# Putting the Fourier stages and W_fourier between the head pairs of attention

## The chip, the cores and the metric

The kernel runs on one NeuronCore of one Trainium2 chip. The metric is the device time of one launch in microseconds; the median of three runs before the change is 1103.17 us (1102.57 to 1104.6).

## What is computed

The reference is a trunk of two layers. Each layer normalizes x (512 positions, 1024 channels), projects it once, and sends the result through two groups side by side: a Fourier group on 512 channels and windowed attention with 8 heads of 64 on 2 key heads. Their outputs are normalized, joined and projected with w_o; a feed-forward network with a short convolution follows. Everything is fp32.

```python
def fourier_mix(u, w_f, b_f):
    f = jnp.fft.fft2(u.astype(jnp.float32), axes=(1, 2), norm="ortho").real.astype(u.dtype)
    return f @ w_f + b_f

for l in range(DEPTH):
    h = rmsnorm(x, norm1[l])
    p = h @ w_in[l]                       # fourier 512 | q 8x64 | k 2x64 | v 2x64
    y_f = fourier_mix(u, w_fourier[l], b_fourier[l])
    q = rope(rmsnorm(q, q_norm[l]))
    k = rope(rmsnorm(k, k_norm[l]))
    y_a = windowed_gqa(q, k, v, sink[l])  # |i-j| <= 128, a sink logit per head
    mix = jnp.concatenate([rmsnorm(y_f, g_fourier_out[l]), rmsnorm(y_a, g_attn_out[l])], axis=-1)
    x = x + mix @ w_o[l]
    h = rmsnorm(x, norm2[l])
    up = dwconv_centred(h @ w_up[l], conv_w[l], conv_b[l])
    gate, val = up[..., :D_FF], up[..., D_FF:]
    x = x + (jax.nn.silu(gate) * val) @ w_down[l]
```

## The kernel before

x lies in SBUF with channels on the partitions, as eight tiles of 128 x 512. TensorE works on fp32r, so every operand is split into a high part (ScalarE, L86) and a low part (VectorE, L89 or L92), and `mm3` (L103 to L108) issues three matmuls for each product: high by high (L106), low by high (L107), high by low (L108). Weights of layer 0 are loaded raw (`wraw`, three buffers) and split on the way (`whi`, `wlo`, five buffers each). Those of layer 1 are split while layer 0 still runs (`presplit`, L135), through `m` and `tA` buffers, stored to DRAM as `kept`, and fetched ready split.

A layer's mixer has these steps, in the order of the program before:

- the projection to q, k, v; then `prep` and `turn_k`, `turn_q` for the keys and the fourth pair of heads (norm, RoPE, and transposes on PE, L423 and L434);
- the projection to the Fourier channels with `W_u` into four PSUM banks `pee` and `poo` (L495 to L511). The input is folded by the symmetry of the transform, so that cosine and sine parts have half the length;
- `prep` and `turn_q` for the other pairs, then `attention` for pairs 3, 0, 1, 2 (L513 to L517), a pair being heads 2p and 2p + 1;
- two Fourier stages (L534 to L566) as matmuls with the tables `th`, `tl` and the alternating row `altr` (L549, L551), each written out to `slab` tiles and a one-row `tail`;
- `W_fourier` (L568 to L597) in four column tiles: in layer 0 a load, a fold on DVE (`tA`), a split, 15 matmuls into `pu` and `pv`, bias on ACT (`tF`), unfolding on DVE, and squares summed in `accF`;
- the norm: `col_rstd` sums over the partitions on PE (L209) and takes the root with 12 small DVE ops (`nv`, `ni`, `nr`, `nq`); `row_rstd` spreads it over the partitions on PE (L216) and copies it to `rb`; then four scalings and four splits to `slab` (`ys`, L599 to L604);
- `w_o` on the Fourier half (96 matmuls, L624 to L627), the norm of the attention half, `w_o` on the attention half.

In `attention`, each head has four blocks of 128 queries. A block takes scores on PE (L459), mask and maximum on DVE (L463), the exponential on ACT, the reciprocal on DVE (L467), the scaling on POOL (L468), transposes on PE (L471) and a split to `pT`; a head ends with 12 matmuls by the values (`vz`). PSUM has eight banks: three `mm`, two `sc` (scores), two `tp` (transposes), one `av` (output). The `tA` ring has six buffers, shared by attention, the folds and `presplit`.

The framework fixes the order on each engine when the program is built: it takes instructions by their place in the program, but lets a later one pass where an earlier one still lacks operands or a buffer in its estimate. Each engine then runs its list strictly in order. Beside this, the matmuls of the Fourier half of `w_o` are tied to attention: the n-th product may not stand ahead of the (12 + n)-th block's transpose:

```python
after = steps[min(STEP0 + nfill[0] // RATE, 31)]
```

Of the kernel before, what the change touches and what calls it, by code (L numbers as in the profile page):

```python
# [37 lines left out]
def encoder_kernel(tc, t):  # L38
# [24 lines left out]
    def nm(s):  # L63
        uid[0] += 1
        return f"{s}_{uid[0]}"

    def f(x):
        return x.bitcast(F32)
# [6 lines left out]
    def psum(tag="mm"):  # L75
        return ps.tile([P, 512], F32, tag=tag, name=nm("ps"), bufs=BANKS[tag])
# [5 lines left out]
    def pair(tag, n=512):  # L82
        return temp(2 * n, tag, F32R).rearrange("p (s q) -> p s q", s=2)

    def act(out, in_, func=AF.Copy, **kw):
        return nc.scalar.activation(out, in_, func, **kw)  # L86
# [7 lines left out]
    def split(hi, lo, src, scale=None, eng=None):  # L94

        if scale is None:
            act(hi, src)
            tt(lo, src, f(hi), ALU.subtract, eng)
        else:
            act(hi, src, scale=scale)  # L100
            stt(lo, src, scale, f(hi), ALU.mult, ALU.subtract)
# [197 lines left out]
    def accum(tag="acc"):  # L299
        return cp.tile([P, 512], F32, tag=tag, name=nm(tag), bufs=1)  # L300
# [28 lines left out]
    for l in range(L):  # L329
# [87 lines left out]
        def turn_q(qs, tag):  # L417

            o = pair(tag)
            for h in range(2):  # L420
                pt = psum("tp")
                for b in range(NB):
                    nc.tensor.transpose(pt[:, b * P:(b + 1) * P], f(qs[:, b, h].rearrange("p s d -> p (s d)")), ident)  # L423
                act(o[:, h, :], pt)
            return o
# [67 lines left out]
        qT = {3: turn_q(qs3, "m4")}  # L493
# [16 lines left out]
                mm3(poo[:, 0:256], [h[:, s, 257:385] for s in range(2)], wo, st, sp_, skip_group_check=True)  # L510
                mm3(poo[:127, 256:512], [h[:, s, 385:512] for s in range(2)], wo, False, sp_, skip_group_check=True)  # L511

        for p, qs in enumerate(prep((0, 1, 2))):  # L513
            qT[p] = turn_q(qs, "act")
        attention(3, True)
        for p in range(3):
            attention(p, False)  # L517

        def tail_out(pe, scale):
            b = tp.tile([1, 2, 258], F32R, tag="tail", name=nm("tail"), bufs=2)  # L520
            split(b[:, 0, :], b[:, 1, :], pe[2][:1, :258], scale=scale)
            return b

        def stage_out(pe, po, scale):
            tiles = []
            for m in range(2):
                a = pair("slab", 514)
                n = P - m
                split(a[:, 0, :258], a[:, 1, :258], pe[m][:, :258], scale=scale)
                split(a[:n, 0, 258:514], a[:n, 1, 258:514], po[:n, m * 256:(m + 1) * 256], scale=scale)  # L530
                tiles.append(a)
            return tiles, tail_out(pe, scale)

        ue, ut = stage_out(pee, poo, 1.0)  # L534
        for stage in range(2):
            pe = [psum() for _ in range(2)]
            po = psum()
            pe.append(psum())
            for m, (c0, c1) in enumerate(((0, 128), (128, 256), (256, 257))):
                o = pe[m][:c1 - c0, :258]  # L540
                for i in range(2):
                    u2 = [ue[i][:, s, :] for s in range(2)]
                    if stage == 0:
                        mm3(o, [z[:, c0:c1] for z in u2], [z[:, 0:258] for z in tab[i]], i == 0, False)
                    else:
                        mm3(o, [z[:, c0:c1] for z in tab[i]], [z[:, 0:258] for z in u2], i == 0, False)
                for s in range(2):
                    if stage == 0:
                        nc.tensor.matmul(o, ut[:, s, c0:c1], altr, start=False, stop=s == 1)  # L549
                    else:  # L550
                        nc.tensor.matmul(o, altr[:, c0:c1], ut[:, s, :], start=False, stop=s == 1)  # L551
            for m in range(2):
                n = P - m
                o = po[:n, m * 256:(m + 1) * 256]
                for i in range(2):
                    kn = P - i
                    u2 = [ue[i][:kn, s, 258:514] for s in range(2)]
                    t2_ = [z[:kn] for z in tab[i]]
                    st = m == 0 and i == 0
                    if stage == 0:  # L560
                        mm3(o, [z[:, 1 + m * P:1 + m * P + n] for z in u2], [z[:, 256:512] for z in t2_],
                            st, i == 1, skip_group_check=True)
                    else:
                        mm3(o, [z[:, 257 + m * P:257 + m * P + n] for z in t2_], u2,
                            st, i == 1, skip_group_check=True)
            ue, ut = stage_out(pe, po, 1.0 if stage == 0 else 1.0 / 512.0)  # L566

        accF = accum("accF")  # L568
        yf = []
# [30 lines left out]
        for j in range(NF):  # L600
            stt(yf[j], yf[j], gF[:, l, j:j + 1], rbF, ALU.mult, ALU.mult)
            a = pair("slab")
            split(a[:, 0, :], a[:, 1, :], yf[j])
            ys.append(a)  # L604


        nfill = [0]
# [181 lines left out]
```

## Time and profile before

| | |
|---|---|
| median of three runs | 1103.17 us |
| profiled execution | 1104.05 us |
| its span, first to last instruction | 1102.2 us |
| mean granted clock of TensorE | 0.989 |
| PE busy | 1064.3 us, 97% |
| DVE busy | 786.7 us, 71% |
| ACT busy | 523.0 us, 47% |
| POOL busy | 87.9 us, 8% |
| DMA | 141.64 MB, 129 GB/s |

Times are microseconds from the start of the span. PE is TensorE's matmul, PEld its weight loads, DVE VectorE, ACT ScalarE, POOL GpSimd, SP the engine that issues the DMAs. A row of the timeline has start, duration, engine, line, operation, output and inputs, the count, and in brackets the idle time ahead of it with what ended it. A row of windows has, for a stretch, each engine's busy time with its count of instructions, then the granted clock, the share of the DMA engines and GB/s. Lines are those of the kernel before.

### The profile page before, as it was taken

The numbers are of one execution on the slowest core, as the hardware profiler recorded it, in microseconds if no ns is written. First come the engines' busy times: TensorE is split into PE (matmuls) and PEld (weight loads), VectorE is DVE, ScalarE is ACT, GpSimd is POOL, SyncE is SP. The second block draws the span as 40 slices with busy tenths as digits, with TensorE's granted clock in tenths as the row PEclk, the third lists the DMA queues.
The fourth block names the chain that finished last, engine by engine and source line by source line (L and its number), as shares of the span: only waits on it lengthen the run. The fifth ranks groups of instructions, "written<-read, shape, count | busy, mean of one in ns | idle before, by whom it ended". The sixth has DMA issues, their size and how long they took to land.

```text
span 1102.2 us, 14846 instructions
## 1 busy us (share of the span) xinstructions
PE 1064.3 (97%) x5187; PEld 891.9 (81%) x5187; DVE 786.7 (71%) x1574; ACT 523.0 (47%) x964; POOL 87.9 (8%) x158
## 2 busy tenths in 40 slices
PE   7988869999999999999999999999999999999998
PEld 7866757888888888888889888888888888888887
DVE  7898965878775867777736979476978435787732
ACT  5638842555454444555622677244554323455421
POOL 1014400000000000000000034000211000010100
PEclk9999969999999999999999999999999999999999
DMA  6312242233337973335955621323232332333241
GB/s 244 109 36 63 70 175 79 94 96 96 96 91 257 386 260 96 98 100 184 372 163 167 234 77 40 124 87 99 93 115 72 98 113 97 99 96 96 79 133 56
DMA packets 58573, 141.64 MB, mean 129 GB/s; under 512 B 6521, under 2 KB 19074, under 8 KB 58498
## 3 DMA queue, kind: packets, MB, share of 16 engines
q1 hardware_dynamic: 58498, 140.69, 39.4%
q8 instruction: 41, 0.67, 0.3%
q14 instruction: 34, 0.28, 0.1%
HBM read 117.60 MB, written 23.07 MB: 128 GB/s over the span
## 4 chain that ended last, share of the span: by engine, by line
PE 86%; DVE 8%; DMA 2%; ACT 2%; issue 1%; POOL 0%; SPq 0%; DVEq 0%; ACTq 0%
PE ps L106 28%; PE ps L108 27%; PE ps L107 27%; DVE tA L463 1%; DMA whi<-kept 1%; PE ps L459 1%; PE ps L471 1%; DVE wlo L89 1%; PE ps L216 1%; DVE pT L89 1%; DVE tF L92 1%; DVE act L89 1%; DMA wraw<-in_w_o_dram 1%; PE ps L209 1%; DVE tA L89 0%
## 5 line engine op out<-in xcount | busy, mean ns | idle before, releaser
L86 ACT ACTIVATE whi<-wraw 128x512 fp32r<-128x512 f32 (+1 forms) x296 | 181.6, 615 | 296.7 <-PE ps L108 283.2
L106 PE MATMUL ps<-act,whi 128*128 128x512 f32 x768 | 298.6, 389 | 0.0
L107 PE MATMUL ps<-act,wlo 128*128 128x512 f32 x768 | 298.6, 390 | 0.0
L108 PE MATMUL ps<-act,whi 128*128 128x512 f32 x768 | 298.0, 389 | 0.0
L89 DVE TENSOR_TENSOR wlo<-wraw,whi 128x512 fp32r<-128x512 f32 (+1 forms) x304 | 218.8, 723 | 96.8 <-ACT whi L86 95.3
L106 PEld LDWEIGHTS ps<-act,whi 128*128 128x128 f32 x768 | 144.2, 188 | 30.0
L108 PEld LDWEIGHTS ps<-act,whi 128*128 128x128 f32 x768 | 144.2, 188 | 29.9
L107 PEld LDWEIGHTS ps<-act,wlo 128*128 128x128 f32 x768 | 144.2, 188 | 29.8
L92 DVE SCALAR_TENSOR_TENSOR tF<-tF,pb,tF 128x511 f32<-128x511 f32 x176 | 135.1, 772 | 10.9 <-ACT tF L86 8.2
L89 DVE TENSOR_TENSOR tF<-ps,rb 128x512 f32<-128x512 f32 x104 | 71.3, 688 | 77.6 <-PE ps L108 66.7
L106 PE MATMUL ps<-slab,whi 128*128 128x512 f32 (+2 forms) x228 | 87.6, 385 | 7.8 <-ACT tF L86 4.9
L107 PE MATMUL ps<-slab,wlo 128*128 128x512 f32 (+2 forms) x228 | 85.9, 377 | 0.0
L108 PE MATMUL ps<-slab,whi 128*128 128x512 f32 (+2 forms) x228 | 85.6, 377 | 0.3 <-DVE slab L89 0.3
L86 ACT ACTIVATE tF<-tF,pb 128x512 f32<-128x512 f32 x88 | 71.6, 816 | 9.8 <-DVE tF L89 2.0
L89 DVE TENSOR_TENSOR x<-x,ps 128x512 f32<-128x512 f32 (+1 forms) x49 | 32.9, 674 | 44.7 <-PE ps L108 44.5
L106 PEld LDWEIGHTS ps<-slab,whi 128*128 128x128 f32 x228 | 43.0, 189 | 17.0 <-ACT tF L86 5.4
L462 POOL COPY tA<-nsink 128x1 f32<-128x1 f32 x64 | 16.6, 260 | 502.2 <-DMA wraw<-in_w_down_dram 418.0
L89 POOL TENSOR_TENSOR tF<-tF,tF 128x512 f32<-128x512 f32 x22 | 30.2, 1375 | 316.8 <-DVE tF L92 309.8
L107 PE MATMUL ps<-pT,wlo 128*128 128x512 f32 (+1 forms) x132 | 51.0, 386 | 0.0
L108 PE MATMUL ps<-pT,whi 128*128 128x512 f32 (+1 forms) x132 | 50.8, 385 | 0.0
L106 PE MATMUL ps<-pT,whi 128*128 128x512 f32 (+1 forms) x132 | 50.8, 385 | 0.0
L468 POOL TENSOR_SCALAR tA<-tA,den 128x256 f32<-128x256 f32 (+1 forms) x64 | 39.9, 626 | 135.0 <-DVE den L467 132.0
(168 smaller groups left out, 1678.9 us busy)
## 6 DMA issues: line engine op xcount, KB each, us to landing
wraw<-in_w_up_dram SPq DMA_DIRECT2D x88, 512.0 KB, 3.5
wraw<-in_w_down_dram SPq DMA_DIRECT2D x32, 512.0 KB, 6.2
kept<-tA SPq DMA_DIRECT2D x56, 256.0 KB, 5.9
whi<-kept SPq DMA_DIRECT2D x28, 256.0 KB, 4.8
wlo<-kept SPq DMA_DIRECT2D x28, 256.0 KB, 2.6
kept<-tA SPq DMA_DIRECT2D x32, 192.0 KB, 4.1
wraw<-in_w_down_dram SPq DMA_DIRECT2D x32, 192.0 KB, 2.4
wraw<-in_w_o_dram SPq DMA_DIRECT2D x8, 512.0 KB, 5.5
```

Of the source, the lines that this page charges most:

```text
L86: return nc.scalar.activation(out, in_, func, **kw)
L89: return (eng or nc.vector).tensor_tensor(out, a, b, op=op)
L92: return nc.vector.scalar_tensor_tensor(out=out, in0=a, scalar=s, in1=b, op0=op0, op1=op1)
L106: nc.tensor.matmul(out, a[0], b[0], start=start, stop=False, **kw)
L107: nc.tensor.matmul(out, a[1], b[0], start=False, stop=False, **kw)
L108: nc.tensor.matmul(out, a[0], b[1], start=False, stop=stop, **kw)
L209: nc.tensor.matmul(pt[:, 2 * b:2 * b + 2], acc[:, b * P:(b + 1) * P], ones2, start=True, stop=True)
L216: nc.tensor.matmul(pt[:, b * P:(b + 1) * P], r[:, b:b + 1].to_broadcast([P, P]), ident, start=True, stop=True)
L459: nc.tensor.matmul(sc[:, :n], qT[p][:, e, i * P:(i + 1) * P], kT[g][:, s, j0 * P:(j1 + 1) * P], start=s == 0, stop=s == 1)
L462: nc.gpsimd.tensor_copy(pr[:, n:n + 1], nsink[:, l, h:h + 1])
L463: nc.vector.tensor_tensor_reduce(out=pr[:, :n], in0=sc[:, :n], in1=mask[:, m0:m0 + n], scale=-1.0 / math.sqrt(HD), scalar=nsink[:, l, h:h ...
L468: nc.gpsimd.tensor_scalar(pr[:, :n], pr[:, :n], den[:, i:i + 1], 1.0, op0=ALU.mult, op1=ALU.mult)
```

## The change

Three blocks change places in the program, in both layers: the head pairs 0 to 2 were all ahead of the Fourier stages; now `prep` and pair 3 stand between the two stages, pair 0 between the second stage and `W_fourier`, and pairs 1 and 2 behind the norm of the Fourier group. The third output of a stage, `pe[2]`, moves from an `mm` bank to an `sc` bank.

```diff
@@ -510,12 +510,6 @@
-        for p, qs in enumerate(prep((0, 1, 2))):
-            qT[p] = turn_q(qs, "act")
-        attention(3, True)
-        for p in range(3):
-            attention(p, False)
-
@@ -533,9 +527,8 @@
         ue, ut = stage_out(pee, poo, 1.0)
         for stage in range(2):
-            pe = [psum() for _ in range(2)]
+            pe = [psum(), psum(), psum("sc")]
             po = psum()
-            pe.append(psum())
...
@@ -564,6 +557,11 @@
             ue, ut = stage_out(pe, po, 1.0 if stage == 0 else 1.0 / 512.0)
+            if stage == 0:
+                for p, qs in enumerate(prep((0, 1, 2))):
+                    qT[p] = turn_q(qs, "act")
+                attention(3, True)
+        attention(0, False)
...
@@ -602,6 +600,8 @@
             ys.append(a)
+        for p in (1, 2):
+            attention(p, False)
```

What the built program makes of it shows at three places. The first is PE in layer 0, where `W_fourier` ends and `w_o` (`slab` by `whi`, 128x512) begins. Before:

```order
L108 MATMUL ps_1803<-slab_1675,whi_1814 128x256
L106 MATMUL ps_1802<-tail_1680,wt_1806 128x258
L107 MATMUL ps_1802<-tail_1680,wt_1806 128x258
L108 MATMUL ps_1802<-tail_1680,wt_1806 128x258
L209 MATMUL ps_2038<-ones_118,acc_536 128x2 x4
L209 MATMUL ps_1842<-ones_118,accF_1683 128x2 x4
L216 MATMUL ps_1863<-ident,nr_1848 128x128 x4
L216 MATMUL ps_2059<-ident,nr_2044 128x128 x4
L106 MATMUL ps_1896<-slab_1871,whi_1888 128x512
```

In the changed program the first matmuls of `w_o` stand here, among the transposes (L471) and the value matmuls (`pT`) of the last head:

```order
L108 MATMUL ps_1733<-pT_1736,vz_122 128x256
L471 MATMUL ps_1833<-ident,tA_1827 128x128 x3
L471 MATMUL ps_1848<-ident,tA_1842 128x128 x3
L106 MATMUL ps_1896<-slab_1565,whi_1888 128x512
L107 MATMUL ps_1896<-slab_1565,wlo_1889 128x512
L106 MATMUL ps_1910<-slab_1565,whi_1892 128x512
L107 MATMUL ps_1910<-slab_1565,wlo_1893 128x512
L106 MATMUL ps_1934<-slab_1565,whi_1926 128x512
L107 MATMUL ps_1934<-slab_1565,wlo_1927 128x512
L106 MATMUL ps_1733<-pT_1809,vz_122 128x256
L107 MATMUL ps_1733<-pT_1809,vz_123 128x256
```

Before, attention and both norms were over when `w_o` began; now the last head and the norm of attention (`acc_536`) are still to come, and twelve `pT` matmuls stand behind the first of `w_o`.

The second place is DVE in layer 0 at the root of the Fourier norm. Before, it ran side by side with that of attention, behind everything else:

```order
L89 TENSOR_TENSOR wt_6975<-wtr_6973,wt_6975 1x128
L89 TENSOR_TENSOR accF_1683<-accF_1683,tF_1839 128x512
L196 TENSOR_SCALAR nv_1847<-ps_1842 128x4
L196 TENSOR_SCALAR nv_2043<-ps_2038 128x4
L197 TENSOR_SCALAR ni_1850<-nv_1847 128x4
L197 TENSOR_SCALAR ni_2046<-nv_2043 128x4
```

Now its steps stand singly among the scores (L463), reciprocals (L467) and splits of heads 5 to 7 in the order of the work:

```order
L89 TENSOR_TENSOR accF_1377<-accF_1377,tF_1533 128x512
L89 TENSOR_TENSOR pT_1656<-ps_1666,pT_1656 128x256
L463 ISA tA_1769,nmax_1734<-ps_1766,pb,nsink 128x384
L463 ISA nmax_1734 128x1
L467 RECIPROCAL den_1735<-den_1735 128x1
L463 ISA tA_1784,nmax_1734<-ps_1781,pb,nsink 128x256
L463 ISA nmax_1734 128x1
L89 TENSOR_TENSOR pT_1656<-ps_1680,pT_1656 128x384
L196 TENSOR_SCALAR nv_1541<-ps_1536 128x4
L467 RECIPROCAL den_1735<-den_1735 128x1
L463 ISA tA_1813,nmax_1807<-ps_1810,pb,nsink 128x256
```

The root moved ahead of the last head and a half, with a head's ops between its steps.

The third place is PE in layer 1 before the change, where `W_fourier` (`ps_7004`, `ps_7039`) already stood among the transposes and scores (L459) of the first heads:

```order
L108 MATMUL ps_7004<-tail_6967,wt_7008 128x258
L471 MATMUL ps_6268<-ident,tA_6262 128x128 x3
L106 MATMUL ps_7039<-slab_6957,whi_7046 128x258
L107 MATMUL ps_7039<-slab_6957,wlo_7047 128x258
L108 MATMUL ps_7039<-slab_6957,whi_7046 128x258
L106 MATMUL ps_7039<-slab_6962,whi_7046 128x258
L107 MATMUL ps_7039<-slab_6962,wlo_7047 128x258
L108 MATMUL ps_7039<-slab_6962,whi_7046 128x258
L459 MATMUL ps_6396<-m_1289_5921,act_6202 128x256 x2
```

With the change it still stands among heads, its end one head later.

## The prediction

> **What bounds the kernel now.** I read the page from the top: span, slices, then the chain that ended last.
>
> ```profile
> span 1102.2 us, 14846 instructions
> ...
> PE   7988869999999999999999999999999999999998
> ...
> PEclk9999969999999999999999999999999999999999
> ...
> PE 86%; DVE 8%; DMA 2%; ACT 2%; issue 1%; POOL 0%; SPq 0%; DVEq 0%; ACTq 0%
> ```
>
> PE carries 86% of the chain, and nearly every slice is 9. The exceptions stand in the first seven slices (0 to 193 us): the mixer of layer 0. The sixth slice (138 to 165 us) has PE at 6 and a clock digit of 6. So I cut this stretch up with the view of windows, at the places where the built order changes: 107.62 is the first score of the third head pair, 128.48 the first fold of W_fourier, 163.98 the first matmul of w_o, 187.29 the end of its Fourier half.
>
> ```profile
> core 0: us, PE busy (x) PEld busy (x) DVE busy (x) ACT busy (x) POOL busy (x), PEclk, DMA share, GB/s
> ...
> 107.62:128.48 20.86, 18.71 (x118) 15.40 (x118) 18.36 (x68) 17.29 (x53) 11.33 (x32) 1.00 0.07 21
> 128.48:144.50 16.02, 13.21 (x87) 11.35 (x87) 16.02 (x40) 12.34 (x29) 1.57 (x2) 1.00 0.64 198
> 144.50:163.98 19.48, 9.82 (x42) 8.93 (x42) 11.11 (x45) 6.70 (x15) 0.00 (x0) 0.56 0.44 162
> 163.98:187.29 23.31, 22.98 (x96) 17.98 (x97) 12.79 (x20) 6.20 (x11) 0.00 (x0) 1.00 0.24 71
> 107.62:167.66 60.04, 45.17 (x260) 38.17 (x261) 49.17 (x155) 38.31 (x99) 12.90 (x34) 0.86 0.34 113
> ```
>
> Four heads of attention take 20.86 us with DVE 88% busy. W_fourier's first half is held by DVE alone (16.02 of 16.02). Then come 19.48 us in which no engine is full, PE works half the time, and at a clock of 0.56. From 163.98 PE is the bound again. The timeline of PE says what it waited for in the third stretch:
>
> ```profile
> 148.40 0.58 PE L106 MATMUL ps<-slab,whi 128*128 128x256 f32 x1 [3.91 <-ACT tF L86]
> ...
> 155.43 1.84 PE L209 MATMUL ps<-ones,accF 128*128 128x2 f32 x8 [1.47 <-DVE accF L89]
> 159.79 3.40 PE L216 MATMUL ps<-ident,nr 128*128 128x128 f32 x16 [2.52 <-DVE nr L92]
> ...
> 163.98 0.50 PE L106 MATMUL ps<-slab,whi 128*128 128x512 f32 x1 [0.79 <-ACT slab L86]
> ```
>
> This is a chain of latencies: W_fourier's last tiles, the sum of squares, the root, its spreading over the partitions (L216), scaling, split. Attention is over by then, so nothing fills PE.
>
> **The change, part by part.** No instruction's work changes; only the order does. I go through the parts.
>
> *The two Fourier stages* (L549, L551 before) hardly move. In the chain of waits they run ahead of the first score's step on DVE:
>
> ```profile
> 73.95 0.50 PE ps L549 x2
> ...
> 84.57 0.48 DVE tA L463
> ```
>
> The scheduler had put them there already, and in the new order they stand there too. Their third output now takes a score bank and its last eight matmuls fall among the first heads. No row shows that; the nearest is a score's wait for PE in the same heads:
>
> ```profile
> 96.71 0.62 DVE L463 CUSTOM_DVE_ANT_0 tA<-ps,pb,nsink 128x384 f32<-128x384 f32 x1 [1.71 <-PE ps L471]
> ```
>
> I bound it by nothing and by another such wait, 1.7 us, and take nothing: eight matmuls of one row are short beside it.
>
> *W_fourier of layer 0* moves from behind the last scores to behind the scores of the second pair. Its folds now start where the third pair's first score stood, so 107.62 is the common starting point. The new goal is the first full w_o operand (the first `slab` split). I count what DVE must do between the two, since it is the fullest engine on the way. Before, from 107.62 to the last slab, it did 49.17 us. From this I take what now stands behind the first slab:
>
> ```profile
> 107.62 0.48 DVE L463 CUSTOM_DVE_ANT_0 tA<-ps,pb,nsink 128x256 f32<-128x256 f32 x1
> ...
> 138.42 0.54 DVE L89 TENSOR_TENSOR pT<-ps,pT 128x384 fp32r<-128x384 f32 x1
> ...
> 144.00 0.54 DVE L89 TENSOR_TENSOR tA<-m,tA 128x384 fp32r<-128x384 f32 x1
> ...
> 148.15 0.74 DVE L92 SCALAR_TENSOR_TENSOR act<-ps,pa,act 128x512 fp32r<-128x512 f32 x1
> ...
> 151.35 0.68 DVE L89 TENSOR_TENSOR acc<-acc,sq 128x512 f32<-128x512 f32 x1
> ...
> 157.31 0.23 DVE L196 TENSOR_SCALAR nv<-ps 128x4 f32<-128x4 f32 x2 [2.02 <-PE ps L209]
> ...
> 159.48 0.24 DVE L92 SCALAR_TENSOR_TENSOR nr<-nq,nr 128x4 f32<-128x4 f32 x2
> 162.51 2.74 DVE L92 SCALAR_TENSOR_TENSOR tF<-tF,pa,rb 128x512 f32<-128x512 f32 x4 [2.78 <-ACT rb L86]
> 165.17 2.49 DVE L89 TENSOR_TENSOR slab<-tF,slab 128x512 fp32r<-128x512 f32 x4
> ```
>
> Five splits for the next layer (5 x 0.54), three slabs (1.87), three `pT` (3 x 0.54), the last pair's scaling and sum (0.74 + 0.68), and one of the two roots that ran side by side from 157.31 to 159.72 (1.2): 8.8 us. Neighbours overlap by some 0.07 us (the row of 162.51 runs to 165.25, the next starts at 165.17), about 0.8 over twelve of them: 8.0. So DVE has 49.17 - 8.0 = 41.2 us of work up to the first slab.
>
> *Its waits* are the unknown, because no trace shows this mix. Lower end 0: the stretch 128.48 to 144.50 had none. Upper end 10.9: what DVE waited in the same rows before (60.04 - 49.17). I take 5.3: the attention's own waits stay (20.86 - 18.36 = 2.5 for four heads, and four heads are still to come), and the chain of the norm keeps its one long wait (2.78 for `rb`), while its other waits now have heads 6 and 7 beside them. First slab: 107.6 + 41.2 + 5.3 = **154.1 us**, instead of 163.98, where its first half sufficed to start w_o. Ends: 148.8 and 159.7.
>
> *What is late next*: w_o's Fourier half now starts before attention ends, and PE takes on work that was over before. Twelve `pT` matmuls stand behind w_o's first, and the norm of attention (two small groups) comes after the Fourier half.
>
> ```profile
> 139.46 0.33 PE L107 MATMUL ps<-pT,vz 128*128 128x384 f32 x1
> 139.63 0.33 PE L108 MATMUL ps<-pT,vz 128*128 128x384 f32 x1
> ...
> 221.48 0.79 PE ps L209 x8
> ...
> 230.82 0.89 PE ps L216 x8
> ```
>
> At 0.17 us from start to start (lower end) to 0.33 (upper), twelve are 2.0 to 4.0 us; I take 2.0, since they stand in a full queue. With 0.79 + 0.89 that is 3.7. Then w_o's half, 23.31 us as before. The later slabs come in time: up to the last `pT` DVE has 1.87 + 2.7 + 1.6 = 6.2 us to do, PE 36 matmuls at 23.31 / 96 = 0.24, 8.7 us. End of the half: 154.1 + 3.7 + 23.3 = 181.1 against 187.29, so **6.2 us gained**; with the ends of the waits and of the `pT`, -1.4 (159.7 + 5.7 + 23.3 = 188.7) to 11.5. From there on PE was full and stays so.
>
> *SP's queue*: the fourth fold tile, the w_o tiles and the small `wtr` loads now go ahead of the fourth `m` load and all stores of the next layer's weights. In the old order the stores stood among them, and DVE once waited for one:
>
> ```profile
> 147.67 0.56 DVE L89 TENSOR_TENSOR tA<-m,tA 128x384 fp32r<-128x384 f32 x1 [2.52 <-DMA kept<-tA]
> ```
>
> This is a part of the 10.9 above. The splits that such a wait holds up now stand behind the first slab, where PE has work.
>
> *Layer 1* has nothing of this to gain:
>
> ```profile
> 585.00:630.00 45.00, 44.15 (x298) 41.23 (x297) 38.32 (x104) 19.75 (x41) 0.00 (x0) 1.00 0.64 213
> 630.00:655.00 25.00, 24.97 (x175) 20.76 (x175) 19.01 (x63) 19.95 (x54) 7.30 (x14) 1.00 0.20 65
> 655.00:681.00 26.00, 23.54 (x145) 19.76 (x146) 24.11 (x86) 20.27 (x54) 12.04 (x28) 1.00 0.07 21
> 681.00:700.00 19.00, 18.81 (x116) 16.73 (x115) 13.94 (x42) 10.91 (x29) 6.19 (x16) 1.00 0.33 111
> ```
>
> PE's idle time is 0.85 + 0.03 + 2.46 + 0.19 = 3.5 us, because its weights come split and W_fourier already stands among heads 0 and 1. The change pushes it one head back, so the stretch without filler (655 to 681, 9% idle) may shift or grow. Bounds: 3.5 gained, or as much again as that stretch costs (2.5) lost; I take 0.
>
> **Sum.** The profiled execution took 1104.05 us (1102.2 of it span); 1104.05 - 6.2 = 1097.9. It stood 0.88 above the median of the runs, 1103.17; the gain from the median gives **1097 us**.
>
> **The rivals.**
>
> *Full cover.* If the heads' ops fill all of DVE's waits, the slab comes at 148.8 and the gain is 11.5: 1092. For it: DVE ran 16 us without a wait in a mix of W_fourier and a head. Against: the norm is a strict chain.
>
> *GpSimd is held up by what now stands beside it.* Each block of probabilities is scaled on POOL (L468) and DVE, ACT and PE wait behind it.
>
> ```profile
> L468 POOL TENSOR_SCALAR tA<-tA,den 128x384 f32<-128x384 f32 (+1 forms) x16 | 8.5, 536 | 5.8 <-DVE den L467 5.8
> ...
> 87.91 0.84 POOL L468 TENSOR_SCALAR tA<-tA,den 128x256 f32<-128x256 f32 x1 [25.18 <-DVE den L467]
> ...
> 89.84 1.23 POOL L468 TENSOR_SCALAR tA<-tA,den 128x384 f32<-128x384 f32 x1 [1.09 <-DVE den L467]
> 90.26 1.40 DVE L89 TENSOR_TENSOR ropetab<-ropetab,pb 128x256 f32<-128x256 f32 x3
> ```
>
> In the stretch of pure attention its mean is 536 ns; beside DVE ops that read two tiles of SBUF it took 0.84 and 1.23. The change brings such ops (folds, `wlo`, slabs) to sixteen of these scalings. At 0.84 - 0.54 = 0.3 each on the path that is 4.8 us: gain 1.4, 1102. Against: the order has only a part of the sixteen beside such an op, and the tiles in flight hide a part. [...]
>
> *The strict queues give it all back (slower).* DVE, ACT and PE run in the order built. W_fourier's chain of fold, high part, low part, matmul, output stands ahead of the third pair's scores, and the twelve small ops of the root are strewn singly among the ops of the last three heads. The last sum of squares ended at 155.3:
>
> ```profile
> 154.59 0.69 DVE L89 TENSOR_TENSOR accF<-accF,tF 128x512 f32<-128x512 f32 x1 [0.56 <-ACT tF L86]
> ```
>
> If each side waits for the other, the heads (20.86) follow W_fourier (128.48 to 155.3, 26.8) and the norm (up to the first slab's end, 165.17 + 2.49 / 4 = 165.8; 10.5) follows both: first slab at 107.6 + 26.8 + 20.9 + 10.5 = 165.8, end at 192.8, 5.5 us late: 1109. It decides from a first slab later than 160.3 (187.29 - 27.0). Against: that is longer than all waits of before together.
>
> *It does nothing*, since the scheduler had interleaved all there was: true of the stages and of layer 1; in layer 0 the order does move W_fourier. 1103.
>
> **How the numbers follow.** Forecast (gain 3 to 9, 1094 to 1100): 0.55. Full cover: 0.15. GpSimd: 0.15. Nothing: 0.06. Slower: 0.09. The range 1091 to 1102.5 holds the first three and leaves out about 0.15. A measurement of this kernel tells 0.2% (2.2 us) from no change. Faster: 0.55 + 0.15 + half of GpSimd's = 0.78; same 0.13; slower 0.09.
>
> **What would show it.** In layer 0: first w_o matmul near 154; PE's clock 1.0 between 140 and 165; no wait of PE over 3 us there; `pT` matmuls among w_o's. The window from the third pair's place to the first slab shows DVE near 41 us busy; what it waits beside that is my 5.3. L468's mean for heads 4 to 7 over 0.7 us speaks for GpSimd; a first w_o later than 160 for the strict queues. Layer 1, from W_in to the end of w_o, should keep its length within 2 us. I am wrong if the gain sits elsewhere, or if DVE still waits for stores.

## The result, and the profile after

| | before | after |
|---|---|---|
| median | 1103.43 us (four runs, 1102.57 to 1104.6) | 1090.57 us (four runs, 1089.6 to 1091.19) |
| profiled execution, its span | 1104.05 us, 1102.2 us | 1089.6 us, 1087.8 us |

The ratio is 0.9879, with a 95% interval from 0.9867 to 0.9891: 12.0 to 14.7 us less. The forecast was 1097 us, with a range from 1091 to 1102.5. The measured time lies 0.4 us below the lower end of that range. The sign and the place were right; the gain by the medians, 12.9 us, was twice the forecast 6.2.

The page of the changed kernel, the same lines as before: span, slices, the chain that ended last.

```profile
span 1087.8 us, 14834 instructions
...
PE   8987999999999999999999999999999999999998
...
PEclk9899999999999999999999999999999999999999
...
PE 85%; DVE 10%; DMA 2%; ACT 2%; issue 2%; POOL 0%; SPq 0%; DVEq 0%; ACTq 0%; POOLq 0%
```

The sixth slice, which had PE at 6 and the clock at 6, now has 9 and 9, and the fifth went from 8 to 9. The fourth (82 to 109 us) came down from 8 to 7: PE waits there for 2.32 us (for ACT) and for 1.68 us (for DVE). Even so, W_fourier's first fold stands at 107.12, 0.5 us ahead of the row that marked the same place before (107.62). The clock's 8 in the second slice lies ahead of all that was moved. The windows, cut at W_fourier's first fold (107.12), at the first slab's low part (147.10) and at the end of w_o's Fourier half (170.78):

```profile
core 0: us, PE busy (x) PEld busy (x) DVE busy (x) ACT busy (x) POOL busy (x), PEclk, DMA share, GB/s
107.12:147.10 39.98, 34.67 (x222) 29.26 (x222) 39.64 (x131) 32.84 (x89) 15.68 (x34) 1.00 0.36 115
147.10:170.78 23.68, 23.30 (x108) 19.20 (x107) 16.45 (x29) 9.28 (x18) 0.00 (x0) 1.00 0.48 161
```

DVE is busy for 39.64 of 39.98 us. The 19.48 us in which no engine was full are gone, and the clock is 1.00 in both stretches. DVE's timeline shows the same at single rows: the scaling by `rb` stood behind a wait of 2.78 us, and now has none; the x sum behind it is the first row that waits for long, for PE.

```profile
107.12 0.76 DVE L89 TENSOR_TENSOR tA<-wraw 128x256 f32<-128x256 f32 x2
...
143.98 2.73 DVE L92 SCALAR_TENSOR_TENSOR tF<-tF,pa,rb 128x512 f32<-128x512 f32 x4
...
147.10 0.68 DVE L89 TENSOR_TENSOR slab<-tF,slab 128x512 fp32r<-128x512 f32 x1
...
155.49 1.89 DVE L89 TENSOR_TENSOR x<-x,ps 128x512 f32<-128x512 f32 x3 [1.97 <-PE ps L108]
```

PE's timeline in the same place: its longest wait is 1.91 us, w_o starts at 145.43 instead of 163.98, and `pT` matmuls of the last heads stand among w_o's.

```profile
140.95 0.88 PE L471 MATMUL ps<-ident,tA 128*128 128x128 f32 x4 [1.91 <-DVE pT L89]
...
145.43 0.51 PE L106 MATMUL ps<-slab,whi 128*128 128x512 f32 x1 [0.31 <-ACT slab L86]
...
147.48 0.39 PE L106 MATMUL ps<-pT,vz 128*128 128x256 f32 x1 [0.38 <-ACT pT L86]
...
155.76 0.34 PE L106 MATMUL ps<-pT,vz 128*128 128x384 f32 x1
```

One landmark serves for every run below, because PE is full ahead of it (busy for 128.88 of 128.88 us from 450.00 on before, for 64.01 of 64.01 from 500.00 on in the changed kernel) and its place in the program never moves: the sum over the partitions for layer 1's first norm, behind layer 0's last product. First the kernel before, then the changed one:

```profile
578.88 0.95 PE L209 MATMUL ps<-ones,acc 128*128 128x2 f32 x8
```

```profile
564.01 0.95 PE L209 MATMUL ps<-ones,acc 128*128 128x2 f32 x8
```

Layer 0 ends 14.87 us earlier. The spans differ by 14.4, so layer 1 and its end lost 0.5. The medians differ by 12.9: the profiled execution of before stood 0.6 above its median, that of after 1.0 below.

### The profile page after: what moved, and what is told of

It reads as the page before. It is cut to its first block, busy times and chain, and to the rows that moved or that the text cites. A ratio compares the mean times of both kernels' runs of the same rounds, so it can differ in the third digit from the quotient of the medians.

```text
span 1087.8 us, 14834 instructions
## 1 busy us (share of the span) xinstructions
PE 1058.9 (97%) x5187; PEld 889.0 (82%) x5187; DVE 785.0 (72%) x1574; ACT 522.4 (48%) x964; POOL 91.0 (8%) x158
## 4 chain that ended last, share of the span: by engine, by line
PE 85%; DVE 10%; DMA 2%; ACT 2%; issue 2%; POOL 0%; SPq 0%; DVEq 0%; ACTq 0%; POOLq 0%
PE ps L106 27%; PE ps L108 27%; PE ps L107 27%; DVE tA L463 1%; DVE act L89 1%; DVE wlo L89 1%; DMA whi<-kept 1%; PE ps L471 1%; PE ps L459 1%; PE ps L216 1%; DVE tA L89 1%; ACT tA L86 1%; DVE tF L89 1%; PE ps L209 1%; DVE pT L89 0%
## 5 line engine op out<-in xcount | busy, mean ns | idle before, releaser
L106 PE MATMUL ps<-act,whi 128*128 128x512 f32 x768 | 298.9, 389 | 0.0
L108 PE MATMUL ps<-act,whi 128*128 128x512 f32 x768 | 297.7, 389 | 0.0
L89 DVE TENSOR_TENSOR wlo<-wraw,whi 128x512 fp32r<-128x512 f32 (+1 forms) x304 | 218.7, 723 | 98.7 <-ACT whi L86 97.1
L108 PEld LDWEIGHTS ps<-act,whi 128*128 128x128 f32 x768 | 144.2, 188 | 29.9
L106 PEld LDWEIGHTS ps<-act,whi 128*128 128x128 f32 x768 | 144.2, 188 | 29.8
L92 DVE SCALAR_TENSOR_TENSOR tF<-tF,pb,tF 128x511 f32<-128x511 f32 x176 | 135.3, 772 | 10.7 <-ACT tF L86 8.0
L89 DVE TENSOR_TENSOR tF<-ps,rb 128x512 f32<-128x512 f32 x104 | 71.2, 689 | 77.2 <-PE ps L108 63.0
L106 PE MATMUL ps<-slab,whi 128*128 128x512 f32 (+2 forms) x228 | 86.7, 381 | 2.2 <-ACT whi L86 1.2
L108 PE MATMUL ps<-slab,whi 128*128 128x512 f32 (+2 forms) x228 | 85.0, 375 | 0.0
L89 DVE TENSOR_TENSOR x<-x,ps 128x512 f32<-128x512 f32 (+1 forms) x49 | 32.8, 675 | 43.6 <-PE ps L108 43.4
L89 POOL TENSOR_TENSOR tF<-tF,tF 128x512 f32<-128x512 f32 x22 | 30.2, 1374 | 316.2 <-DVE tF L92 309.2
L468 POOL TENSOR_SCALAR tA<-tA,den 128x256 f32<-128x256 f32 (+1 forms) x64 | 42.3, 665 | 130.9 <-DVE den L467 130.5
L106 PEld LDWEIGHTS ps<-slab,whi 128*128 128x128 f32 x228 | 42.8, 188 | 11.0 <-ACT whi L86 1.6
L108 PE MATMUL ps<-pT,whi 128*128 128x512 f32 (+1 forms) x132 | 50.8, 385 | 0.0
L106 PE MATMUL ps<-pT,whi 128*128 128x512 f32 (+1 forms) x132 | 50.8, 385 | 0.0
```

The source lines that it names most:

```text
L89: return (eng or nc.vector).tensor_tensor(out, a, b, op=op)
L92: return nc.vector.scalar_tensor_tensor(out=out, in0=a, scalar=s, in1=b, op0=op0, op1=op1)
L106: nc.tensor.matmul(out, a[0], b[0], start=start, stop=False, **kw)
L108: nc.tensor.matmul(out, a[0], b[1], start=False, stop=stop, **kw)
L468: nc.gpsimd.tensor_scalar(pr[:, :n], pr[:, :n], den[:, i:i + 1], 1.0, op0=ALU.mult, op1=ALU.mult)
```

## The experiments

For the runs, the mixer's steps were written as a list of jobs per layer: `out`, `s0`, `s1` (the first output and the two stages), `prep`, the pairs 3, 0, 1, 2, `wf` (W_fourier) and `norm` (its norm and slabs). With the two lists of before and after it builds the same orders as the two kernels. Line numbers in rows of these runs are higher by two to six (L92 for L89; L108 or L109 for L106). The kernel before gave medians from 1103.46 to 1104.74 in the four groups of runs, so runs of different groups are compared by their ratio to it, which is given with its 95% interval. A trace shows one execution, and the traced ones stood between 1.5 us below and 0.8 above the median of their kernel (one pair later: 2.9 above), so differences of 1 to 2 us between two traces are within this.

**Which layer.**

```diff
-layer 0: out s0 prep 3 s1 0 wf norm 1 2
+layer 0: prep 3 0 1 2 out s0 s1 wf norm
 layer 1: out s0 prep 3 s1 0 wf norm 1 2
```

> The new order in layer 1 alone; layer 0 keeps the order of before. Theory (all of the gain is W_fourier among the heads of layer 0, and layer 1 loses the 0.5 us that the two traces show there): the time of before or up to 1 us more, 1103 to 1104.5. Rival (layer 1 has a share of the gain which the traces hide by other shifts): 1097 to 1101.

1104.72 us, ratio 1.0014 (1.0004 to 1.0023), 0.2 us beyond the theory's range and far from the rival's. All of the gain is in layer 0.

**Which part of the change.** In both layers, the stages alone, with the third output in a score bank:

```diff
-prep 3 0 1 2 out s0 s1 wf norm
+out s0 prep 3 s1 0 1 2 wf norm
```

> In both layers the stages stand where the change puts them, third output in a score bank, but W_fourier and its norm stand behind all heads as before. Theory (W_fourier's place is what counts): 1102 to 1105, within 2 us of before. Rival (the stages' early place frees the banks and lets W_fourier's work come forward): 1091 to 1098.

1105.96 us, 1.0030 (1.0017 to 1.0043): the stages' move by itself costs 2.5 us, 1 us more than the theory allowed; layer 0 ended at 580.67, 1.8 later. Then W_fourier alone, in both layers, with the banks as before:

```diff
-prep 3 0 1 2 out s0 s1 wf norm
+prep 3 0 out s0 s1 wf norm 1 2
```

> The stages keep their banks and stand behind two pairs of heads in the program; W_fourier and its norm stand between pair 0 and pair 1 as in the change. Theory: the whole gain, 1089 to 1092.5. Rival (the gain needs the stages' new place too): 1095 to 1103.

1093.57 us, 0.9919 (0.9904 to 0.9934): most of the gain, but 3 to 4 us short of the whole, between the two expectations. DVE's timeline of this run, and the first product of w_o on PE, show where they stay:

```profile
144.90 0.56 DVE L92 TENSOR_TENSOR tA<-m,tA 128x384 fp32r<-128x384 f32 x1 [0.89 <-DMA kept<-tA]
...
147.45 0.56 DVE L92 TENSOR_TENSOR tA<-m,tA 128x384 fp32r<-128x384 f32 x1 [0.46 <-DMA kept<-tA]
```

```profile
149.58 0.50 PE L109 MATMUL ps<-slab,whi 128*128 128x512 f32 x1 [0.99 <-ACT slab L89]
```

Seven splits for layer 1 (`tA<-m`) stand ahead of the first slab, where the changed kernel has three, and two of them wait for a store. So I asked what these splits cost, by ordering them behind the last slab:

```diff
-                split(two[0], two[1], src)
+                with tc.issue_after(hold[0].ins), tc.issue_after(hold[1].ins):
+                    split(two[0], two[1], src)
...
-                    split(a[:, 0, :], a[:, 1, :], yf[j])
+                    hold[:] = split(a[:, 0, :], a[:, 1, :], yf[j])
```

In the kernel before:

> The kernel before, with the splits of layer 1's weights (tA<-m) ordered behind the last slab of layer 0's norm. Ahead of it stood eight of them (0.47 us from start to start) and VectorE's wait of 2.52 us for one of their stores. Theory (these are a part of what the change moved out of the way): first slab 3 to 6 us earlier, 1097.5 to 1100.5. Rival (W_fourier's own chain and the norm's are what the slab waits for): 1102 to 1104.

1099.67 us, 0.9964 (0.9951 to 0.9977). Layer 0 ended at 573.18, 5.7 earlier. The long waits of the norm's chain were all still there (first two rows, DVE; the last row is PE's):

```profile
151.63 0.23 DVE L200 TENSOR_SCALAR nv<-ps 128x4 f32<-128x4 f32 x2 [2.82 <-PE ps L213]
...
156.83 2.74 DVE L95 SCALAR_TENSOR_TENSOR tF<-tF,pa,rb 128x512 f32<-128x512 f32 x4 [2.79 <-ACT rb L89]
```

```profile
158.30 0.50 PE L108 MATMUL ps<-slab,whi 128*128 128x512 f32 x1 [0.43 <-ACT slab L89]
```

So some 4 to 6 us could be had without the change, by this alone. In the run of W_fourier alone, and in the changed kernel:

> W_fourier and norm between pairs 0 and 1, the stages as before (the run that gave 1093.6), now with the splits of layer 1's weights held behind the last slab. In that run seven of them stood ahead of the first slab, where the changed kernel has three, and VectorE waited 1.4 us for their stores. Theory (this is the whole difference between that run and the changed kernel, the stages' place gives nothing itself): 4 to 6 us under 1093.6, 1087.5 to 1089.5, like the changed kernel with the same hold or up to 1.7 less. Rival (the stages' place is what gives the 3 us): 1090.5 to 1093.

> The changed kernel with the splits of layer 1's weights (tA<-m) held behind layer 0's last slab. Three of them stood ahead of the first slab, with 0.15 us of waits. Theory: 1.4 to 1.6 us earlier, 1088.5 to 1090. Rival (the held splits only move their work to a place where it delays something else): 1090.5 to 1093.

0.9873 (0.9858 to 0.9888; 1090.29 us) and 0.9882 (0.9867 to 0.9897; 1091.46 us). The first lies between its two expectations in microseconds, and by its ratio (0.9873 of 1103.5 is 1089.5) at the edge of the theory's. With the splits held, W_fourier alone is as fast as the changed kernel. So the 3 us were not the stages' own work but the splits that the order happened to put ahead of the slab. For the changed kernel the hold gave nothing, against the theory: VectorE had 1.1 us less to do up to the first slab (39.23 us for 40.32) and waited 1.1 us more (1.44 for 0.34).

**How many heads as cover.** Layer 0's W_fourier one pair later, then one pair earlier than in the change:

```diff
-layer 0: out s0 prep 3 s1 0 wf norm 1 2
+layer 0: out s0 prep 3 s1 0 1 wf norm 2
```

> The changed kernel with layer 0's W_fourier and norm one pair later: behind pair 1, with pair 2 alone to cover them. Theory (VectorE's work up to the first slab sets its time, and the waits stay filled): first slab later by the work of two heads, 9.2 us, at about 157; gain against before 15 - 9.2 and about 1 us for the pT matmuls that no longer stand behind, so 6 to 8 us: 1095 to 1098. Rival 1 (two heads are too few to fill the norm's chain, and the 5.3 us of waits that the prediction took come back): 1100 to 1103. Rival 2 (any head beside it will do, TensorE's whole work decides): 1090 to 1092.

```diff
-layer 0: out s0 prep 3 s1 0 wf norm 1 2
+layer 0: out s0 prep 3 s1 wf norm 0 1 2
```

> The changed kernel with layer 0's W_fourier and norm one pair earlier: behind pair 3, with pairs 0, 1 and 2 to cover them. Theory (VectorE's work up to the first slab sets its time as long as heads fill the waits): first slab 9.2 us earlier, near 138.6, and TensorE has w_o's products to fill its remaining idle time of 5.3 us between 107 and 147: 2 to 5 us under the changed kernel, 1086 to 1088.5. Rival (the second stage ends near 98, so W_fourier cannot start that early, and the heads wait behind it): 1090 to 1094.

One pair later: 1100.44 us, 0.9981 (0.9968 to 0.9995), within the first rival's range. The ten executions lie far apart, from 1098.75 to 1105.96, and the traced one is among the slower (1103.38). DVE's row for the scaling by `rb`, PE's first product of w_o, and two windows:

```profile
157.24 2.74 DVE L95 SCALAR_TENSOR_TENSOR tF<-tF,pa,rb 128x512 f32<-128x512 f32 x4 [1.71 <-ACT rb L89]
```

```profile
158.71 0.79 PE L109 MATMUL ps<-slab,whi 128*128 128x512 f32 x1 [0.64 <-ACT slab L89]
```

```profile
core 0: us, PE busy (x) PEld busy (x) DVE busy (x) ACT busy (x) POOL busy (x), PEclk, DMA share, GB/s
106.86:160.66 53.80, 42.95 (x247) 37.07 (x246) 47.11 (x145) 39.07 (x100) 16.78 (x35) 0.87 0.38 126
158.70:164.00 5.30, 5.29 (x13) 4.14 (x14) 5.05 (x16) 1.89 (x3) 0.00 (x0) 0.50 0.00 0
```

DVE waited 53.80 - 47.11 = 6.7 us up to the end of the first slab: with one pair the forecast's waits (5.3) are there. Besides, w_o ran its first 5.3 us at a clock of 0.50: its products stood 0.43 us apart there and 0.23 behind it (from 164.22 on), which makes some 2.4 us more for the twelve up to 163.98 (5.27 us against 0.34 + 11 x 0.23). Layer 0 ended at 576.01, 2.8 later than in the held run of before, though w_o started within 0.4 us of it. In that run the mean clock up to w_o's slabs was 0.87 too (106.60 to 159.49) and the sums over the partitions ahead of w_o took as long (1.87 and 1.85 us; here 1.71 each), but w_o's products stood 0.23 us apart from the second on. So the half clock in w_o belongs to this execution; that every execution of this order pays it is not shown, and the median, 2.9 us below the traced time, suggests otherwise.

One pair earlier: 1088.43 us, 0.9868 (0.9853 to 0.9883), at the edge of the theory's range. That is 2.1 us under the changed kernel's median, 1.2 by the ratios, and the two intervals overlap. w_o started 5.4 us earlier (139.98), but layer 0 ended only 0.8 earlier (563.21).

**The clock.** In before, the clock stood at 0.56 from 144.5 to 163.98. Matmuls that nothing reads fill that stretch:

```diff
+    def ballast(after, n):
+        o = psum("sc")
+        with tc.issue_after(after):
+            for i in range(n):
+                nc.tensor.matmul(o, tab[0][0][:, :P], tab[1][0], start=i == 0, stop=i == n - 1)
```

> The kernel before, with matmuls on constant tables that nothing reads, in four groups of 10 to 12 between 144 and 164 us, so that TensorE is hardly idle there. Theory (the clock of 0.5 from about 146 to 162.7 lengthens the norm's chain: two L209 groups of 1.87 for 0.95, L216 3.40 for 2.1, the last W_fourier tile): clock near 1.0 and first w_o matmul 2 to 4 us earlier, 1099.5 to 1101.5. Rival (the clock falls where TensorE is off the chain, and costs nothing): 1102.5 to 1104.5.

1106.3 us, 1.0027 (1.0015 to 1.0039): slower, against the theory and above the rival's range too. Windows and PE's timeline (L311 is the ballast):

```profile
core 0: us, PE busy (x) PEld busy (x) DVE busy (x) ACT busy (x) POOL busy (x), PEclk, DMA share, GB/s
144.50:156.00 11.50, 7.53 (x45) 6.00 (x43) 9.07 (x20) 6.42 (x15) 0.00 (x0) 1.00 0.81 280
156.00:165.02 9.02, 9.02 (x45) 7.67 (x45) 4.70 (x28) 2.03 (x4) 0.00 (x0) 0.81 0.01 2
```

```profile
155.73 1.02 PE L213 MATMUL ps<-ones,accF 128*128 128x2 f32 x8 [2.65 <-DVE accF L92]
156.61 4.57 PE L311 MATMUL ps<-th,th 128*128 128x512 f32 x12
161.02 1.05 PE L222 MATMUL ps<-ident,nr 128*128 128x128 f32 x8
```

With a full clock up to 156 the sum over the partitions (L209, here L213) took 1.02 us instead of 1.84 (at 0.50, 155.40 to 157.30), and the root on DVE began at 156.79 instead of 157.31, though the last sum of squares came 0.3 us later. Behind it the ballast itself held up the spreading (L222 begins only when the 12 matmuls end), so the rest of the chain was not measured, and the run meets neither expectation. What the low clock adds to the chain before can be estimated from rows: 0.8 us in L209, and 1.0 in the spreading (from the first L216 to `rb` 2.1 us before, 1.1 in the changed kernel), 1.8 us in all. This is a part of VectorE's 10.9 us of waits. In the run above the low clock stood inside w_o, where PE was busy for 5.29 of 5.30 us and had no idle time to take it up.

**VectorE's work.** More of it in the changed kernel:

```diff
                        w = wsplit(wf_raw)
+                        for _ in range(2):
+                            tt(w[1][:, :512], wf_raw, f(w[0])[:, :512], ALU.subtract)
```

> The changed kernel, with each low part of layer 0's four W_fourier tiles computed three times: eight more VectorE instructions of 0.67 us (0.61 from start to start) ahead of the first slab. Theory (VectorE is full from 107 to the first slab, so its work sets the slab's time): 4.9 us later, 1094.5 to 1096. Rival (VectorE only looks full, latencies of other engines set the slab): 1090.5 to 1092.5.

And less of it, with the splits held:

```diff
-                        w = wsplit(fold_wf(wload(t["w_fold"][l, j], 1024)))
+                        w = wsplit(wload(t["w_fold"][l, j], 1024)[:, :512])
```

> The changed kernel with the splits of layer 1's weights held behind the last slab (the run that gave no gain), and the eight folds of layer 0's W_fourier left out: the first half of each tile is split unfolded, so the Fourier half's values are not the reference's. VectorE has 2.9 us less to do ahead of the first slab. Theory A (VectorE's work alone sets the slab): 2 to 3 us under the held run's 0.9882 of before, 1087 to 1089. Theory B (two limits stand close together: VectorE's work of 38 to 40 us, and the chain of the heads' blocks, which the norm's small instructions stand among; less work comes back as waits for ACT and TensorE): within 1.2 us of the held run, 1089.5 to 1092, with over 2 us of waits on VectorE between 107 and the first slab.

More: 1097.06 us, 0.9944 (0.9929 to 0.9959). The first slab began at 156.30, 9.2 later. Of that, 7.2 are VectorE's work (4.9 added, 1.4 for three more splits that the new order put ahead of it, 3 x 0.47, and 0.9 for other instructions that changed places, three `pT` among them), 0.9 waits, and 1.2 a later first fold. The time paid 6.5 of the 9.2 us (7.2 by the ratios). That is more than the theory's range and far from the rival's: more work on VectorE is paid for.

Less: 1091.06 us, 0.9881 (0.9867 to 0.9896), the same as the held run's 0.9882. The number is that of theory B, and VectorE's waits came back as it said: 3.2 us between 107 and the end of the first slab. But w_o began far earlier than either theory said, and layer 0 ended no earlier:

```profile
137.78 0.50 PE L108 MATMUL ps<-slab,whi 128*128 128x512 f32 x1
...
565.06 0.95 PE L213 MATMUL ps<-ones,acc 128*128 128x2 f32 x8
```

w_o starts 8.9 us ahead of the held run's 146.63, and layer 0 ends 0.6 us behind its 564.43. The edit took 2.9 us of work away, but the built order moved more: up to the end of the first slab VectorE is busy for 30.70 us, against 39.23 in the held run, because five low parts of w_o's weights now stand behind it, one low part of W_fourier ahead of 107, and four `pT` fewer in between. So here an earlier first slab was worth nothing. A likely reason is that little is left on PE to fill: it is busy for 77.21 of the 83 us from 107 to 190 in the changed kernel, 77.90 in the held run and 79.35 in this one (there at a mean clock of 0.98, in the other two at 1.00). No run separates this from the work that was pushed behind the slab.

**GpSimd.** The prediction's rival in two forms: layer 0's folds moved there (`eng` is `nc.gpsimd`), and its scaling doubled.

```diff
-    def fold_wf(raw):
+    def fold_wf(raw, eng=None):
...
-        tt(w[:, :256], raw[:, :256], raw[:, 512:768], ALU.add)
+        tt(w[:, :256], raw[:, :256], raw[:, 512:768], ALU.add, eng)
```

> The changed kernel with the eight folds of layer 0's W_fourier tiles (tA<-wraw, 2.9 us of VectorE) on GpSimd. Theory (VectorE's work sets the first slab): up to 2.9 us earlier, 1088 to 1089.5. Rival (GpSimd is held up by VectorE's instructions beside it, and the folds stand ahead of the scalings of the probabilities there): 1091 to 1095, with L468's mean between 107 and 147 us well over the 698 ns of the changed kernel.

```diff
+                    if l == 0 and p < 3:
+                        nc.gpsimd.tensor_scalar(pr[:, :n], pr[:, :n], ones2[:, 0:1], 1.0, op0=ALU.mult, op1=ALU.mult)
                     nc.gpsimd.tensor_scalar(pr[:, :n], pr[:, :n], den[:, i:i + 1], 1.0, op0=ALU.mult, op1=ALU.mult)
```

> The changed kernel with a second GpSimd instruction of L468's form (times 1.0, in place) ahead of each L468 of pairs 0 to 2 in layer 0; VectorE's order is the same row for row. It adds some 0.55 to 0.7 us to the chain of each of 24 blocks, three to four times what the changed neighbours added to L468 (0.16 us). Theory (tiles in flight hide it; that is why the prediction's GpSimd rival cost nothing): at most 2 us more than the changed kernel, 1090 to 1093. Rival (GpSimd is on the path and the 0.16 us a block were paid): 16 of these blocks lie between 107 and the first slab, so 8 us or more, over 1098.

Folds: 1093.77 us, 0.9905 (0.9889 to 0.9922), against 0.9879 (0.9867 to 0.9891) for the changed kernel: no faster, against the theory, and by the middle values slower. A fold takes twice what it took on DVE (830 ns for 414), and W_fourier's first low part comes 3.1 us late (112.55 for 109.45). First the group on POOL, then DVE's row for the first low part:

```profile
L92 POOL TENSOR_TENSOR tA<-wraw 128x256 f32<-128x256 f32 x8 | 6.5, 830 | 0.5 <-PE ps L474 0.4
```

```profile
112.55 1.23 DVE L92 TENSOR_TENSOR wlo<-tA,whi 128x512 fp32r<-128x512 f32 x1 [0.89 <-ACT whi L89]
```

The number is the rival's, its sign is not: the scaling's mean was not over 698 ns but 617 (11.1 us for 18). The price of the late tile is not isolated, since five splits for layer 1 stood ahead of the slab here instead of three, one of them behind a wait of 1.82 us.

Scaling doubled: 1093.16 us, against 1091.70 us for the changed kernel beside it. The groups on POOL between 107 and 148:

```profile
L473 POOL TENSOR_SCALAR tA<-tA,den 128x384 f32<-128x384 f32 x10 | 6.8, 684 | 0.1
L473 POOL TENSOR_SCALAR tA<-tA,den 128x256 f32<-128x256 f32 x9 | 6.8, 753 | 1.0 <-DVE den L470 0.8
L472 POOL TENSOR_SCALAR tA<-tA,ones 128x384 f32<-128x384 f32 x10 | 6.0, 602 | 1.1 <-ACT tA L89 1.1
L472 POOL TENSOR_SCALAR tA<-tA,ones 128x256 f32<-128x256 f32 x9 | 4.7, 523 | 2.6 <-ACT tA L89 2.5
```

The added instructions took 10.7 us on these 19 blocks (24 in all), and the time rose by 1.5 us, with intervals that overlap (0.9900, 0.9885 to 0.9915, for 0.9883, 0.9866 to 0.9899): the blocks in flight hide nearly all of it.

**Beside each other.** The changed kernel, and the fastest variant, which puts W_fourier behind pair 3, keeps layer 0's banks as before and holds the splits:

```diff
-layer 0: out s0 prep 3 s1 0 wf norm 1 2
+layer 0: prep 3 out s0 s1 wf norm 0 1 2
 layer 1: out s0 prep 3 s1 0 wf norm 1 2
```

> Layer 0: stages with the banks of before, W_fourier and norm behind pair 3 alone, splits held; layer 1 as changed. Theory (what the earlier pair gave, 2 us, and what the hold gives, 1.5 us, add up until TensorE's work between 84 and 175 us is the bound): 1086 to 1088.5. Rival (TensorE is already the bound with the earlier pair, and the hold gives nothing more): 1088 to 1090.

> The changed kernel once more, its jobs written as a table but in the same built order row for row, as the measure for the other runs beside it on the same chip: 1089.5 to 1092.

> The fastest kernel so far once more, beside the changed kernel on the same chip: 1086.5 to 1088, 2.5 to 4 us under the changed kernel.

The variant gave 1087.44 us, 0.9848 (0.9833 to 0.9862), and 1087.75 us, 0.9849 (0.9834 to 0.9863) in the second group; there the changed kernel gave 1091.70 us, 0.9883 (0.9866 to 0.9899). The variant is 4.0 us under it, and w_o starts at 138.21. The changed kernel's second profile is a warning: same built order, but layer 0 ended at 566.43, 2.4 us later than in the first. The first split for layer 1 was already 1.3 later (142.85 for 141.56), and a store that the first did not show held DVE up by 1.0:

```profile
145.91 0.56 DVE L92 TENSOR_TENSOR tA<-m,tA 128x384 fp32r<-128x384 f32 x1 [1.04 <-DMA kept<-tA]
```

The runs in which W_fourier or the splits change places, by the start of w_o, all times in us. First matmul and end of layer 0 are of the traced execution, the ratio of all:

| run | pairs behind W_fourier in layer 0 | splits ahead of the first slab | first w_o matmul | end of layer 0 | ratio |
|---|---|---|---|---|---|
| before | 0 | 8 | 163.98 | 578.88 | 1 |
| one pair later | 1 | 8 | 158.71 | 576.01 | 0.9981 |
| before, splits held | 0 | 0 | 158.30 | 573.18 | 0.9964 |
| W_fourier alone | 2 | 7 | 149.58 | 567.48 | 0.9919 |
| W_fourier alone, held | 2 | 0 | 147.54 | 564.83 | 0.9873 |
| changed, held | 2 | 0 | 146.63 | 564.43 | 0.9882 |
| changed | 2 | 3 | 145.43 | 564.01 | 0.9879 |
| one pair earlier | 3 | 0 | 139.98 | 563.21 | 0.9868 |
| earlier, held | 3 | 0 | 138.40 | 561.97 | 0.9848 |
| no folds, held | 2 | 0 | 137.78 | 565.06 | 0.9881 |

## Why the prediction was right in sign and short in size

The forecast gain was 6.2 us, and the traced executions differ in layer 0 by 14.87. The step that failed is the sum for the start of w_o: VectorE's waits were taken at 5.3 us and came to 0.34, and the end of the first slab was taken for the start of w_o. The mechanism, heads that fill the norm's chain, was right; the prediction had it work only by half.

*What bounds before, and where*: right. The gain is in layer 0's mixer (the run with layer 1 alone), by W_fourier's place (the runs with each part alone), and PE is full from w_o on.

*The stages at nothing, up to 1.7 us*: right once W_fourier has moved too: with the splits held, W_fourier alone and the whole change differ by less than their intervals. The eight matmuls that the forecast called short took 1.2 us (96.00 to 97.19 in the changed kernel, 0.28 each). By themselves the stages cost 2.5 us (1.9 to 4.7 by the interval), beyond the bound.

*VectorE's work, 41.2 us*: 39.64 + 0.68 = 40.3 us. The start was 107.12, 0.5 earlier than assumed. Together 1.4 us of the miss.

*VectorE's waits, 5.3 us of a possible 10.9*: **the term that failed**. From 107.12 to the end of the first slab, 147.78, are 40.66 us: 0.34 us of waits, 5.0 us less than taken. The step kept the 2.5 us of the heads' own waits and the 2.8 us for `rb`, as if heads and norm did not fill each other's gaps. They do: the waits were 10.9 us with no pair behind W_fourier (9.8 with the splits held, so it is not the splits that make the difference) and 6.7 with one. With two they were 0.34 here, 1.5 in the second profile of the same order, 1.4 with its splits held, and 2.1 and 3.8 in the runs of W_fourier alone, without and with the hold. So 0.34 is the lowest of five, and all five lie under the 5.3 of the forecast. The rival "full cover", given 0.15, was the right one.

*First slab as the start of w_o*: **the second term that failed**, a slip of bookkeeping. 154.1 is the end of the first slab's low part, 163.98 the start of the first matmul, which needs the high part only. In before the two lie 1.87 us apart (165.17 + 0.68 - 163.98), in the changed kernel 2.35 (147.78 - 145.43). The full-cover rival had the same slip: without it, 11.5 becomes 13.4 to 13.9.

*What comes late, 3.7 us*: right. The sum's other part, from the first matmul of w_o to the end, was 27.0 us (23.3 + 3.7); 187.29 - 14.87 - 145.43 is 27.0. PE shows the parts where they were expected: the twelve `pT` matmuls among w_o's, and the two groups of attention's norm with 0.80 and some 1.0 us behind w_o's Fourier half.

The terms add up: 6.2 + 0.5 + 0.9 + 5.0 + 2.35 = 14.95, measured 14.87 between the two traced executions. The medians differ by 12.9 only. Of the 2.0 between, 0.5 was lost in layer 1, and 1.5 is where these two executions stood to their medians, so the terms may be too large by as much.

*The splits for the next layer*: counted as work that moves behind the slab, five of eight, which is what happened (three stay). Not foreseen was how much hangs on it: in before, holding them is worth 4 to 6 us by itself. Of the change's gain, W_fourier's place is worth some 10 us with the splits held on both sides (0.9964 to 0.9873).

*GpSimd held up, 1102*: the rows came, the price did not. The scaling's mean in this stretch went from 536 to some 700 ns:

```profile
L468 POOL TENSOR_SCALAR tA<-tA,den 128x384 f32<-128x384 f32 x9 | 7.1, 784 | 2.5 <-DVE den L467 2.4
L468 POOL TENSOR_SCALAR tA<-tA,den 128x256 f32<-128x256 f32 x9 | 5.5, 609 | 4.0 <-DVE den L467 3.8 <-PE ps L471 0.2
```

This 0.16 us a block is far less than the 0.56 that the doubled scaling added for 1.5 us in all. Five of the 18 make it up: 1.00 us at 107.25 beside `tA<-wraw` on DVE, 1.55 at 123.09 and 1.24 at 132.07 beside `accF<-accF,tF`, 0.96 at 127.81 beside `wlo<-wraw,whi`, 0.88 at 141.51 beside `tA<-m,tA`, all of them ops that read two tiles of SBUF. The other 13 took 0.58 to 0.60 us (128x384) or 0.48 (128x256), also the one at 109.17, with `wlo<-tA,whi` beside it from 109.45 on. The longer rows did not decide the time.

*Strict queues, 1109*: nothing of it. *Layer 1 within 2 us*: right, 0.5.

What stays open: how the 0.5 us of layer 1 come about (with its new order alone it was 0.2 faster in the profile), what the half clock costs the norm's chain behind the root, since the ballast got in its way (1.0 us is an estimate from rows), and what limits layer 0 once w_o starts ahead of 146.

## What to carry to other kernels

A strict chain (a norm, a root, a spreading) with an engine that waits in it is best placed among independent work; count how many blocks of that work fit behind it, and take most of the waits as gone once they outlast the chain: here four heads sufficed (0.3 to 3.8 us of waits left) and two did not (6.7 us). Compare like with like when a start is shifted: the operand half that really releases the next engine, not the end of the whole. And look at what fills an engine "for free" ahead of a chain: work for a later layer that waits for its own stores was not free here (4 to 6 us in the kernel before).

## What the runs showed of the hardware

- The low clock showed its price in two places. In the norm's chain the sum over the partitions took 1.84 us at a clock of 0.50, and 1.02 with the ballast ahead of it (1.00 up to 156). In w_o, with one pair later, PE was busy for 5.29 of 5.30 us at 0.50 and the products stood 0.43 us apart; in before, at 1.00, they stand 0.23 apart. For twelve of them this makes some 2.4 us.
- After sums over the partitions that took about as long ahead of w_o (1.71 and 1.85 us), w_o's products stood 0.43 us apart for 5.3 us in one execution, and 0.23 from the second product on in another.
- The same built order gave layer 0 ends 2.4 us apart (564.01 and 566.43), 1.3 us of it already at the first split for layer 1, and 1.04 by a wait for a store; a single profile of this kernel is not exact to 0.2%.
- GpSimd took 830 ns for a two-input fold of 128x256 that takes VectorE 414 ns.
